# Forgetting attention: the value products of two heads in one group, alternating between the halves of the columns

## The chip, the cores and the metric

The kernel runs on one core of a Trainium2 chip. The metric is the time of one execution on the device in microseconds. The engines are TensorE (PE in the profile, its weight loads PEld), VectorE (DVE), ScalarE (ACT), GpSimd (POOL) and SyncE (SP), which issues most transfers.

## What is computed

The reference is one layer of a decoder trunk on 1024 tokens of width 1024: four token mixers side by side (RWKV-7, a convolution module, gated linear attention, forgetting attention), each projected up, gated and summed; then cross-attention and a SwiGLU feed-forward network. The change is in the forgetting attention (4 heads of width 64). Cut to what matters:

```python
qh = heads(f_q) * (FOX_HEAD_DIM ** -0.5)
kh, vh = heads(f_k), heads(f_v)
c = jnp.cumsum(log_f, axis=1).transpose(0, 2, 1)
for i in range(T // FOX_BLOCK):                 # 8 blocks of 128 queries
    q0, q1 = i * FOX_BLOCK, (i + 1) * FOX_BLOCK
    logits = jnp.einsum('bhtd,bhsd->bhts', qh[:, :, q0:q1], kh[:, :, :q1])
    logits = logits + c[:, :, q0:q1, None] - c[:, :, None, :q1]
    probs = softmax(where(mask, logits, -inf))  # causal
    outs.append(jnp.einsum('bhts,bhsd->bhtd', probs, vh[:, :, :q1]))
```

Query block i sees i + 1 key blocks of 128.

## The kernel before

Activations lie transposed, channels on partitions, in blocks of 128. Most matrix products are done in three products of high and low parts (`mm3`, L171, L174, L175), on 128 x 128 weights and 512 tokens. The products of the small mixers are plain float32.

**The heads.** `fox` (L862) works on two pairs of heads, p = 0 and 1. A pair's two heads, u = 0 and 1, have their values side by side in the columns of `vr` (fvr in the profile): columns 0 to 63 for u = 0, 64 to 127 for u = 1. `head` (L895) is a generator for 128 queries of one head in three steps:

- scores: three products (and a fourth, L907, for the causal mask) into `ps_fs`; then the softmax on VectorE and ScalarE: maximum (L911), its negation (L914), exponential with its sum (L917), reciprocal (L920), normalisation (L921) into `fp`;
- transposes: 128 x 128 blocks of `fp` on TensorE (L928, tile `ps_ft`), copied to `fpt` by ScalarE (L929);
- values: for each key block one product (L935) with a stationary operand of 128 rows and 64 columns, which lands in 64 partitions of `ps_fo`. Four query blocks of both heads share one bank, which ScalarE copies out (L939).

**What sets the order.** Sixteen such generators (8 query blocks, the two heads in turn) are run three deep: in step n the unit n - 2 does its values, n - 1 its transposes, n its scores, in this order on TensorE. `weave` (L204) puts FOX_PIECES = 4 pieces of fill ahead of each step. The fill is `gates` (L984): the gate and up projections of the branches that are finished, six matmuls a piece, with their weights' transfer (SP), cast (`whi`, ScalarE, L153) and low part (`wlo`, VectorE, L154). `queued` keeps a step's products behind the fill given out before. Inside these limits the framework's scheduler orders each engine's instructions.

**A place of the same shape.** In the gated linear attention, L784 forms the intra-chunk outputs: for each of four token blocks, one product for the head in columns 0 to 63 and one for the head in columns 64 to 127, in turn (tile `ps_oi`). Each of them is a sum by itself; nothing is added up over several.

`fp`, `fpt`, the queries, keys and values of a pair of heads share a pool of nine buffers (`pB`).

Of the kernel before, what the change touches and what calls it, by code (L numbers as in the profile page):

```python
# [22 lines left out]
P = 128  # L23
# [3 lines left out]
TH = 512  # L27
# [8 lines left out]
# blocks of w_in, in the order in which they are packed  # L36
# [5 lines left out]
# columns of the per-channel parameters  # L42
# [9 lines left out]
# columns of the constants  # L52
# [39 lines left out]
def hybrid_kernel(ctx, tc, io, out):  # L92
# [17 lines left out]
    def gps(name, shape=(P, TH), both=True):  # L110
        """one of four banks; the last two are left out unless both"""
        bank[0] = 1 - bank[0] if both else 0
        return psg.tile(list(shape), F32, tag=("g", "g2")[bank[0]], name=name)

# [49 lines left out]
    def mm3(ps, pairs, start=True, stop=True, lag=99):  # L164
        """ps (+)= sum of the products of (lhs hi, lhs lo, rhs hi, rhs lo), each exact to f32.

        The products of hi parts run lag pairs ahead of the others."""
        n = len(pairs)
        for i in range(n + min(lag, n)):
            if i < n:  # L170
                mm(ps, lhsT=pairs[i][0], rhs=pairs[i][2], start=start and i == 0, stop=False)  # L171
            if i >= min(lag, n):
                lh, ll, rh, rl = pairs[i - min(lag, n)]
                mm(ps, lhsT=ll, rhs=rh, start=False, stop=False)  # L174
                latest[0] = mm(ps, lhsT=lh, rhs=rl, start=False, stop=stop and i == n + min(lag, n) - 1)  # L175
        return latest[0]
# [3 lines left out]
    def queued():  # L180
        """what the tensor engine is given here comes after the products that were last given to it"""
        return tc.issue_after(latest[0].ins)

    def drain(gen, n=None):
        """n more steps of gen (all that are left when n is None)"""
        while n is None or n > 0:
            if next(gen, gen) is gen:
                return
            n = n if n is None else n - 1
# [4 lines left out]
    def both(gens):  # L194
        """two generators of two steps, side by side"""
# [8 lines left out]
    def weave(fill, streams, n=1, idle=0, gate=None):  # L204
        """the streams' steps in turn, behind n pieces of fill each; then idle more of these.

        A step that gives out a number waits until gate() has reached it."""
# [21 lines left out]
    def rstd(srcs, col, alloc, op, const, minus=(), order=ExitStack):  # L229
        """1/sqrt of op(sum over channels of srcs, const), in PSUM, on all channels; the square of the  # L230
        sum over channels of minus is taken off first.

        srcs [P, w] add up, col [P, heads] holds the channels' weights per head (a head is P // heads
        partitions). The root is taken with the tokens on partitions, and refined by a Newton step.
        In two steps.
        """
# [35 lines left out]
    # the tensor engine's clock rises while the first loads are under way  # L272
# [18 lines left out]
    def project(src, evac, w=None, pieces=1, both=True):  # L291
        """a block of x's projections, in pieces of each half's product"""
# [12 lines left out]
    # shifted r, k, v: per half [P, pair, TH]; the others over all tokens  # L305
# [29 lines left out]
    def rwkv(t1, ps1, fill):  # L335
# [9 lines left out]
        # lower-triangular score matrices, transposed; what lies outside the mask stays zero  # L345
# [4 lines left out]
        # DRAM images of [P, 4, P] matrices in which the 16 x 16 diagonal blocks have one stride  # L350
# [19 lines left out]
        def score(alloc, dst, m, ks, qs, cs, name):  # L370
            """masked scores of the four heads, keys on partitions"""
# [10 lines left out]
        def prepare(hf):  # L382
            """what a half needs before its state: a generator of steps; a step's number is given out
            first where it is about to write the chunk's scores"""
# [27 lines left out]
            # kmod takes the place of k, rk that of the squares, nb that of a  # L412
# [9 lines left out]
            # decays; kk, nb, kmod and r are scaled in place  # L422
# [4 lines left out]
            def scale(c):  # L427
                cs = slice(c * P, (c + 1) * P)
                q = pp([P, 2, 256], "ps_ce")
                # exact: the constants are 0 and +-1  # L430
# [25 lines left out]
            # inverses of I minus the diagonal blocks (both orientations)  # L456
# [15 lines left out]
        # heads are kept in the order h = 2 * (half of the partitions) + pair  # L472
        def chunk(hf, c, r, kk, nb, kmod, v, y, ecl, bm):
            """a chunk of 128 tokens in CHUNK steps"""
# [8 lines left out]
            # (I - A)^-1 and its transpose: blocks of 16 to 32, to 64, to 128  # L483
# [27 lines left out]
            # rows  # L511
# [35 lines left out]
            # U0 | W  # L547
# [29 lines left out]
            # next state  # L577
# [11 lines left out]
            # outputs, transposed  # L589
# [13 lines left out]
        def chunks(hf, args):  # L603
            """the chunks of a half; a chunk's first steps go with the last two of the one before"""
# [13 lines left out]
        def finish(hf, rk, v, xg, misc, y):  # L618
            # normalisation over a head's channels
# [12 lines left out]
            for p in range(2):  # L632
                # bonus, then the output gate
# [54 lines left out]
    def log_sigmoid(dst, x, tmp):  # L688
        """dst = min(x, 0) - log(1 + exp(-|x|))"""
# [172 lines left out]
    def fox(t2, ps2, c_d):  # L862
        for p in range(2):
# [21 lines left out]
            # three heads under way: scores, their transposes, the values  # L885
            zo = [None, None]
            units = [head(p, u, i, qa[u], ka[u], vr, zo, t2, ps2) for i in range(8) for u in range(2)]
# [7 lines left out]
    def head(p, u, i, qa, ka, vr, zo, t2, ps2):  # L895
        """128 queries of a head, in three steps"""
        n = (i + 1) * P
        qs = slice(i * P, n)
        us = slice(64 * u, 64 * u + 64)
# [24 lines left out]
        for j0 in range(0, i + 1, 4):  # L924
# [4 lines left out]
            nc.scalar.copy(pt[:, j0:j0 + m], z[:, 0:m])  # L929
        yield  # L930
        if u == 0 and i % 4 == 0:
            zo[i // 4] = ps2.tile([P, 4, P], F32, tag="gi", name="ps_fo", bufs=2)
        z = zo[i // 4]
        for j in range(i + 1):
            mm(z[us, i % 4], lhsT=vr[:, j, us], rhs=pt[:, j], start=j == 0, stop=j == i)  # L935
        if u == 1 and i % 4 == 3:
# [44 lines left out]
    merged = []  # L981

    def gates(br, t2):
        """a branch's part of the merge, in pieces"""  # L984
# [71 lines left out]
    class HL:  # L1056
        """hi and lo parts of a transposed activation, 8 blocks of [P, TH], of one half of the tokens."""
# [14 lines left out]
    class Norm:  # L1072
        """LayerNorm over the 1024 channels (8 blocks x partitions) of some of the tokens, in place.

        add(j) is called when block j is there; steps(sink) then goes on in small steps and calls
        sink(j, ap) after each block. eng adds up over the blocks.
        """
# [12 lines left out]
        def square(self, j, c, first):  # L1090
            """centre block j, square it; all but the first square are added to the first"""
# [18 lines left out]
        def steps(self, sink):  # L1110
            """a step for the mean, 8 for squares, one for the root, 8 for what is left"""
# [13 lines left out]
    class LastNorm(Norm):  # L1125
        """The same where nothing follows that could hide it: blocks are centred by the mean c of the
        first two as soon as that is known, and the variance is mean((x - c)^2) - mean(x - c)^2; its two
        terms are at most 4 and 3 times the variance, since c is the mean of a quarter of the channels."""
# [18 lines left out]
        def finish(self, dst):  # L1147
            last, acc = KD - 1, self.acc
            # the table of the root is loaded ahead of the need
# [21 lines left out]
    # w_out and the first norm; the norm of one half goes with the products of the next  # L1171
# [14 lines left out]
    # keys and values of mem, in units of one or two blocks of weights  # L1186
# [3 lines left out]
    def memory():  # L1190
# [9 lines left out]
        def load(n):  # L1200
            h, g = units[n]
            # more blocks are under way where w_out has made room
# [7 lines left out]
        for n, (h, g) in enumerate(units):  # L1210
# [11 lines left out]
            else:  # L1222
# [5 lines left out]
                # one bank, two sums: only its first product clears what is written  # L1228
# [37 lines left out]
    # cross-attention; a head's output takes the place of its queries  # L1266
    qh = [HL(pA, "A", "qA"), HL(pM, "M", "qB")]

    def attend(hf, h):
        """in steps; each step is sent the matrix product behind which its own are to queue"""  # L1270
# [34 lines left out]
    def gemms(items):  # L1305
        """output blocks of half the tokens, two pieces each: first pieces, then second pieces"""
# [47 lines left out]
    def run_head(unit, gen, n):  # L1354
        """the steps of a head, with n pieces of gen before each"""
# [37 lines left out]
    # SwiGLU; x2 accumulates alpha * x2 + its output  # L1393
# [5 lines left out]
    def ffn_up(f, sls, ws, steps=(0, 0)):  # L1399
        """the numbers of steps of side to go on after each of the two products"""  # L1400
# [16 lines left out]
    def ffn_down(fs, ws, sls, ln=None):  # L1417
        """adds the products of some blocks; those with the last block wait for a second output block"""
# [45 lines left out]
    # the last blocks by slices of the tokens, so that the norm of one goes with the products of the next  # L1464
# [22 lines left out]
def _pack(inp):  # L1487
# [30 lines left out]
    def tiles(m):  # L1518
        """[K, F] -> [F/128, 128, K/128 * 128]: the stationary blocks, contiguous."""
# [8 lines left out]
    # [4 heads * 2, 128, (4 k, 256)]  # L1528
# [3 lines left out]
    # [branch, 8 j, 128, (2 k, 128)]  # L1532
# [46 lines left out]
```

## Time and profile before

| | |
|---|---|
| timed runs, median of 3 | 2235.68 us (2231.76 to 2238.44) |
| span of the profiled execution, first to last instruction | 2235.5 us |
| TensorE busy | 2195.0 us, 98% |
| VectorE, ScalarE, GpSimd busy | 51%, 33%, 9% |
| value products of the forgetting attention (L935) | 144 products, which are 288 matmuls |
| from their first to their last start | 651.3 to 929.1 us |

The profiled execution has no time of its own beside its span; the runs were timed apart from it. Matmuls are pipelined, so the duration of one (start to end) is longer than the distance to the next start, and the sum of durations of a line is not its cost. What a group of matmuls costs is read from the starts: of the instruction before it, of its first, and of the instruction behind it.

### The profile page before, as it was taken

What the parts mean: (1) busy time and instruction counts of PE and PEld (TensorE: products, weight loads), DVE (VectorE), ACT (ScalarE), POOL (GpSimd) and SP (SyncE); (2) the same over time, 40 slices, a digit from 0 to 9 for tenths busy, and PEclk for the clock granted to TensorE, in tenths of its full rate; (3) what the DMA queues carried; (4) which work ended last, traced back from release to release, by engine and by line L of the source; (5) the groups of instructions that cost most, each with busy time, mean ns of one, the idle gap of its engine ahead of it and who ended that gap; (6) DMA issues with size and microseconds to landing.
All of it is one profiled execution on the core that took longest, in us unless ns stands there. A gap on an engine that the chain in (4) does not pass through costs nothing.

```text
span 2235.5 us, 28264 instructions
## 1 busy us (share of the span) xinstructions
PE 2195.0 (98%) x11468; PEld 1794.7 (80%) x11468; DVE 1149.8 (51%) x2004; ACT 727.2 (33%) x1165; POOL 209.6 (9%) x173
## 2 busy tenths in 40 slices
PE   9999999999999999999999999989999999999997
PEld 7878777777787878888888888877888888888787
DVE  4365287524444433333466346775455455445577
ACT  3343111126646555422234333342111111111223
POOL 0000000000001111121024000150000000000122
PEclk9999999999999999999999999999999999999999
DMA  6122121122211211111444102331111111111421
GB/s 205 48 74 82 51 85 49 62 100 89 62 56 60 68 56 41 37 55 48 132 130 149 43 29 95 99 99 57 48 57 47 48 47 53 51 38 58 148 78 48
DMA packets 87682, 161.08 MB, mean 72 GB/s; under 512 B 19606, under 2 KB 43848, under 8 KB 87552
## 3 DMA queue, kind: packets, MB, share of 16 engines
q1 hardware_dynamic: 87552, 159.28, 22.3%
q8 instruction: 90, 1.47, 0.3%
q14 instruction: 40, 0.33, 0.0%
HBM read 134.50 MB, written 24.76 MB: 71 GB/s over the span
## 4 chain that ended last, share of the span: by engine, by line
PE 91%; issue 3%; DVE 2%; POOL 2%; ACT 1%; DMA 1%; SPq 0%; DVEq 0%; POOLq 0%; ACTq 0%
PE ps_w L174 10%; PE ps_w L175 10%; PE ps_w L171 9%; PE ps_gate L171 5%; PE ps_gate L175 5%; PE ps_gate L174 5%; PE ps_g L171 4%; PE ps_g L175 4%; PE ps_g L174 4%; PE ps_q L174 2%; PE ps_q L175 2%; PE ps_q L171 2%; PE ps_fo L935 2%; PE ps_up L171 1%; PE ps_up L175 1%
## 5 line engine op out<-in xcount | busy, mean ns | idle before, releaser
L153 ACT CAST whi<-wraw 128x1024 fp32r<-128x1024 f32 x189 | 197.9, 1048 | 338.4 <-issue 212.5
L154 DVE TENSOR_TENSOR wlo<-wraw,whi 128x1024 fp32r<-128x1024 f32 x164 | 212.8, 1298 | 158.5 <-ACT whi L153 157.2
L175 PE MATMUL ps_gate<-xl,whi 128*128 128x512 f32 x512 | 200.8, 392 | 0.0
L174 PE MATMUL ps_gate<-xh,wlo 128*128 128x512 f32 x512 | 200.6, 392 | 0.0
L1431 DVE TENSOR_TENSOR x<-x,ps_w 128x512 f32<-128x512 f32 (+1 forms) x306 | 189.1, 673 | 11.0 <-PE ps_w L175 10.6
L171 PE MATMUL ps_gate<-xh,whi 128*128 128x512 f32 x512 | 165.4, 403 | 0.0
L174 PE MATMUL ps_g<-xh,wlo 128*128 128x512 f32 x400 | 158.3, 396 | 0.0
L175 PE MATMUL ps_g<-xl,whi 128*128 128x512 f32 x400 | 158.2, 396 | 0.0
L174 PE MATMUL ps_w<-x2B,wlo 128*128 128x512 f32 (+1 forms) x416 | 147.4, 365 | 3.6 <-POOL wlo L154 3.5
L175 PE MATMUL ps_w<-x2B,whi 128*128 128x512 f32 (+1 forms) x416 | 147.1, 364 | 0.0
L171 PE MATMUL ps_g<-xh,whi 128*128 128x512 f32 x400 | 140.4, 416 | 2.9 <-ACT xh L153 2.8
L175 PE MATMUL ps_w<-hl,whi 128*128 128x512 f32 (+1 forms) x384 | 140.9, 372 | 1.9 <-DVE hl L154 1.7
L174 PE MATMUL ps_w<-hh,wlo 128*128 128x512 f32 (+1 forms) x384 | 141.0, 372 | 0.0
L174 PE MATMUL ps_w<-x2A,wlo 128*128 128x512 f32 x352 | 137.5, 391 | 0.0
L175 PE MATMUL ps_w<-x2A,whi 128*128 128x512 f32 x352 | 137.4, 390 | 0.0
L154 POOL TENSOR_TENSOR wlo<-wraw,whi 128x1024 fp32r<-128x1024 f32 x25 | 63.2, 2528 | 776.4 <-ACT whi L153 770.4
L171 PE MATMUL ps_w<-hh,whi 128*128 128x512 f32 (+1 forms) x384 | 133.1, 372 | 1.0 <-ACT hh L153 1.0
L1414 DVE TENSOR_TENSOR hs<-hs,ps_w 128x512 f32<-128x512 f32 (+1 forms) x48 | 30.8, 642 | 177.2 <-PE ps_w L175 177.0
L174 PEld LDWEIGHTS ps_gate<-xh,wlo 128*128 128x128 f32 x512 | 96.6, 189 | 21.0 <-issue 0.6
L175 PEld LDWEIGHTS ps_gate<-xl,whi 128*128 128x128 f32 x512 | 96.6, 189 | 20.5
L171 PEld LDWEIGHTS ps_gate<-xh,whi 128*128 128x128 f32 x512 | 93.5, 190 | 20.5 <-issue 3.5
L1022 POOL TENSOR_TENSOR merged<-merged,gsig 128x512 f32<-128x512 f32 x48 | 66.1, 1376 | 406.2 <-DVE gsig L1021 301.0
(457 smaller groups left out, 4402.9 us busy)
## 6 DMA issues: line engine op xcount, KB each, us to landing
wraw<-ffn_w SPq DMA_DIRECT2D x84, 512.0 KB, 3.5
wraw<-wblk SPq DMA_DIRECT2D x57, 512.0 KB, 3.6
wraw<-xa_wo SPq DMA_DIRECT2D x16, 512.0 KB, 3.5
xraw<-xT SPq DMA_DIRECT2D x16, 256.0 KB, 6.1
yld<-y_d SPq DMA_DIRECT2D x16, 256.0 KB, 2.5
uraw<-ups SPq DMA_DIRECT2D x32, 128.0 KB, 2.9
wraw<-w_out SPq DMA_DIRECT2D x8, 512.0 KB, 3.5
xr<-xT SPq DMA_DIRECT2D x16, 256.0 KB, 4.4
```

Of the source, the lines that this page charges most:

```text
L153: nc.scalar.copy(hi, src)
L154: eng.tensor_tensor(out=lo, in0=src, in1=hi.bitcast(F32), op=ALU.subtract)
L171: mm(ps, lhsT=pairs[i][0], rhs=pairs[i][2], start=start and i == 0, stop=False)
L174: mm(ps, lhsT=ll, rhs=rh, start=False, stop=False)
L175: latest[0] = mm(ps, lhsT=lh, rhs=rl, start=False, stop=stop and i == n + min(lag, n) - 1)
L935: mm(z[us, i % 4], lhsT=vr[:, j, us], rhs=pt[:, j], start=j == 0, stop=j == i)
L1022: nc.gpsimd.tensor_tensor(out=mj, in0=mj, in1=sg, op=ALU.add)
L1414: tt(out=s, in0=s, in1=p[1], op=ALU.mult)
L1431: tt(out=x2[j][:, sl], in0=x2[j][:, sl], in1=ps, op=ALU.add)
```

## The change

`head` for u = 0 no longer does its values: it leaves its transposed probabilities in a list `pts`, and its third step is empty. The third step of u = 1 does the values of both heads: key block by key block, first the product of u = 0 into partitions 0 to 63, then that of u = 1 into partitions 64 to 127. The products, their operands, their sums and the bank are the same; comments and empty lines aside, nothing else is edited.

```diff
-            zo = [None, None]
-            units = [head(p, u, i, qa[u], ka[u], vr, zo, t2, ps2) for i in range(8) for u in range(2)]
+            zo, pts = [None, None], [None, None]
+            units = [head(p, u, i, qa[u], ka[u], vr, zo, pts, t2, ps2) for i in range(8) for u in range(2)]
...
-    def head(p, u, i, qa, ka, vr, zo, t2, ps2):
+    def head(p, u, i, qa, ka, vr, zo, pts, t2, ps2):
...
-        us = slice(64 * u, 64 * u + 64)
...
+        pts[u] = pt
         yield
-        if u == 0 and i % 4 == 0:
+        if u == 0:
+            yield
+            return
+        if i % 4 == 0:
             zo[i // 4] = ps2.tile([P, 4, P], F32, tag="gi", name="ps_fo", bufs=2)
         z = zo[i // 4]
         for j in range(i + 1):
-            mm(z[us, i % 4], lhsT=vr[:, j, us], rhs=pt[:, j], start=j == 0, stop=j == i)
-        if u == 1 and i % 4 == 3:
+            for w in range(2):
+                us = slice(64 * w, 64 * w + 64)
+                mm(z[us, i % 4], lhsT=vr[:, j, us], rhs=pts[w][:, j], start=j == 0, stop=j == i)
+        if i % 4 == 3:
```

On TensorE, in the first pair of heads, the steps with the values of the seventh query block (7 key blocks; `ps_ft` are the transposes of the next unit, `ps_fs` the scores of the one after, `ps_gate` the fill; L941 is the product line of the changed kernel):

```order
@@ -2248,5 +2242,4 @@
 L174 MATMUL ps_gate<-xh,wlo 128x512
 L175 MATMUL ps_gate<-xl,whi 128x512
-L935 MATMUL ps_fo<-fpt,fvr 64x128 x7
 L928 MATMUL ps_ft<-cst,fp 128x128 x7
 L171 MATMUL ps_fs<-fkh,fqh 128x512
@@ -2278,5 +2271,5 @@
 L174 MATMUL ps_gate<-xh,wlo 128x512
 L175 MATMUL ps_gate<-xl,whi 128x512
-L935 MATMUL ps_fo<-fpt,fvr 64x128 x7
+L941 MATMUL ps_fo<-fpt,fvr 64x128 x14
 L928 MATMUL ps_ft<-cst,fp 128x128 x8
 L171 MATMUL ps_fs<-fkh,fqh 128x512
```

The group of the first head is gone and its transposes' neighbours stand directly behind the fill; the group of the second head has twice as many products. It is the same at all eight query blocks of both pairs.

The scheduler also moves some instructions of the other engines. On VectorE, in the second pair of heads, ahead of the softmax of the last unit (u = 1, 8 key blocks), before:

```order
L154 TENSOR_TENSOR ul<-uraw,uh 128x256
L911 TENSOR_REDUCE fst<-ps_fs 128x1 x2
L154 TENSOR_TENSOR wlo<-wraw,whi 128x1024
L913 TENSOR_TENSOR fst<-fst 128x1
L914 TENSOR_SCALAR fst<-fst 128x1
```

A weight's low part stands between the two maxima and their joining. In the changed kernel, at the same place:

```order
L154 TENSOR_TENSOR ul<-uraw,uh 128x256
L154 TENSOR_TENSOR wlo<-wraw,whi 128x1024
L911 TENSOR_REDUCE fst<-ps_fs 128x1 x2
L913 TENSOR_TENSOR fst<-fst 128x1
L914 TENSOR_SCALAR fst<-fst 128x1
```

The weight's low part has moved ahead of the maxima. In each pair of heads there are two more places at which a weight's low part now stands ahead of a part of the softmax, both at the fourth query block.

## Rows read from the trace of the kernel before

**Rows 1.** The page: busy time, share of the span, instructions.
```profile
PE 2195.0 (98%) x11468; PEld 1794.7 (80%) x11468; DVE 1149.8 (51%) x2004; ACT 727.2 (33%) x1165; POOL 209.6 (9%) x173
```

**Rows 2.** Stretches: length, busy time of each engine (instructions), granted clock, transfers.
```profile
core 0: us, PE busy (x) PEld busy (x) DVE busy (x) ACT busy (x) POOL busy (x), PEclk, DMA share, GB/s
636.00:930.00 294.00, 294.00 (x1527) 237.06 (x1526) 114.50 (x248) 170.75 (x278) 37.77 (x29) 1.00 0.16 50
1216.00:1226.40 10.40, 7.36 (x46) 5.89 (x45) 9.44 (x12) 6.07 (x10) 7.71 (x7) 1.00 0.70 232
1226.40:1233.20 6.80, 5.88 (x25) 5.69 (x26) 4.82 (x6) 0.99 (x2) 3.09 (x2) 0.50 0.34 114
```

**Rows 3.** The tile ps_fo: ns min/median/max, first and last start, forms.
```profile
L935 PEld LDWEIGHTS ps_fo<-fpt,fvr x288: 132/137/137, 651.3 to 929.0; 128*64 128x64 f32 x144
L935 PE MATMUL ps_fo<-fpt,fvr x288: 272/273/323, 651.3 to 929.1; 128*64 128x128 f32 x144
```

**Rows 4.** Order of time, TensorE, 918 to 923: start, us, instruction.
```profile
918.75 0.39 PE L175 MATMUL ps_up<-yl,uh 128*128 128x512 f32 x1
919.07 1.96 PE L935 MATMUL ps_fo<-fpt,fvr 128*64 128x128 f32 x16
920.96 1.09 PE L928 MATMUL ps_ft<-cst,fp 128*128 128x128 f32 x8
```

**Rows 5.** Order of time, TensorE, transposes without value products ahead.
```profile
644.97 0.39 PE L175 MATMUL ps_up<-yl,uh 128*128 128x512 f32 x1
645.21 0.27 PE L928 MATMUL ps_ft<-cst,fp 128*128 128x128 f32 x1
```

**Rows 6.** Chain of waits, 860 to 935: start, us, what.
```profile
864.27 1.24 PE ps_fo L935 x10
...
919.14 1.89 PE ps_fo L935 x16
```

**Rows 7.** Order of time, TensorE, the gated linear attention's alternating products.
```profile
578.70 0.39 PE L174 MATMUL ps_gate<-xh,wlo 128*128 128x512 f32 x1
578.93 0.39 PE L175 MATMUL ps_gate<-xl,whi 128*128 128x512 f32 x1
579.25 1.09 PE L784 MATMUL ps_oi<-scm,kv 128*64 128x128 f32 x16
580.27 0.73 PE L171 MATMUL ps_gate<-xh,whi 128*128 128x512 f32 x2
```

**Rows 8.** Order of time, VectorE, softmax at 4, 6 and 8 key blocks.
```profile
837.93 0.49 DVE L921 TENSOR_SCALAR fp<-fp,fst 128x512 f32<-128x512 f32 x1
...
845.59 0.58 DVE L921 TENSOR_SCALAR fp<-fp,fst 128x512 f32<-128x512 f32 x1
...
880.07 0.62 DVE L921 TENSOR_SCALAR fp<-fp,fst 128x768 f32<-128x768 f32 x1
...
914.26 1.22 DVE L154 TENSOR_TENSOR wlo<-wraw,whi 128x1024 fp32r<-128x1024 f32 x1
...
918.98 0.75 DVE L921 TENSOR_SCALAR fp<-fp,fst 128x1024 f32<-128x1024 f32 x1
```

**Rows 9.** Order of time, TensorE, the transposes of these units.
```profile
840.87 0.66 PE L928 MATMUL ps_ft<-cst,fp 128*128 128x128 f32 x4
...
848.75 0.66 PE L928 MATMUL ps_ft<-cst,fp 128*128 128x128 f32 x4
...
882.93 0.87 PE L928 MATMUL ps_ft<-cst,fp 128*128 128x128 f32 x6
```

**Rows 10.** The page: weights' cast and split (mean ns), transfer (KB, us to landing).
```profile
L153 ACT CAST whi<-wraw 128x1024 fp32r<-128x1024 f32 x189 | 197.9, 1048 | 338.4 <-issue 212.5
L154 DVE TENSOR_TENSOR wlo<-wraw,whi 128x1024 fp32r<-128x1024 f32 x164 | 212.8, 1298 | 158.5 <-ACT whi L153 157.2
...
wraw<-wblk SPq DMA_DIRECT2D x57, 512.0 KB, 3.6
```

**Rows 11.** Order of time, SyncE, 905 to 916: the transfer's issue.
```profile
915.50 0.33 SPq L158 DMA_DIRECT2D wraw<-wblk  x1
```

## The prediction

> **What bounds the kernel now.** I read the page's busy shares first. TensorE is busy for 98% of the span [rows 1]; the reader is to see that no other engine comes near. That share is an average, so I next took the busy times of the stretch in which the forgetting attention runs, 636 to 930 us: TensorE is busy for all 294.00 of its 294 us, at the full 2.4 GHz (granted clock 1.00), VectorE for 114.50, ScalarE for 170.75 [rows 2]. Whatever TensorE is spared there comes off the end, as long as nothing else becomes late.
>
> Then the products of probabilities and values themselves. A float32 product is two weight loads and two matmuls, so the 144 products of this line are 288 matmuls; each takes 272 to 273 ns from start to end [rows 3], but they are pipelined, and what counts is the distance between starts. In the order of time, the last group of the second pair of heads that has transposes behind it (8 key blocks, 16 matmuls) starts 0.32 us behind the start of the matmul before it, and the transposes behind it start 1.89 us later [rows 4]. Where no such group stands in between, the transposes start 0.24 us behind the same kind of matmul [rows 5]. So a group of 8 blocks costs 0.32 + 1.89 - 0.24 = 1.97 us. The chain of waits gives the slope: a group of 10 matmuls takes 1.24 us, one of 16 takes 1.89 [rows 6], hence 0.65 / 6 = 0.108 us a matmul, 0.217 a key block. A group of m blocks costs 0.234 + 0.217 m: the constant is the price of going over from full-width products to half-width ones and back, the rest is the streaming.
>
> **What two halves in alternation cost.** This kernel already has such a place: the intra-chunk products of the gated linear attention (L784), which alternate between columns 0 to 63 and 64 to 127 with the same operand shapes (128 x 64 stationary, 128 x 128 moving, float32). At full clock 16 of them start 0.32 us behind the matmul before, and the next matmul starts 1.02 us after their first [rows 7]. The 16 in one half took 1.89 [rows 4]. With 0.23 us, the usual distance of that stream (578.70 to 578.93 [rows 7]), taken off, the alternating 16 cost 0.32 + 1.02 - 0.23 = 1.11 us, and the formula with m = 4 gives 1.10: four blocks of two heads for the price of four blocks of one. The two halves run side by side.
>
> The Trainium skill, page "TensorE: Matmul & The Clock Gate", section "Part 3: Packing small matmuls — row/col tiling", says that a weight load overlaps matmuls in flight only where its row group differs; here all loads use all 128 rows. By that rule a pair of loads (137 ns [rows 3]) would stand ahead of its pair of matmuls. The trace disagrees: eight pairs of loads, each pair 137 ns, are 1.10 us by themselves, and the 16 alternating products with all their loads took 1.02 [rows 7]. What the rule would make of the time is the third rival.
>
> **The sum.** Against the profiled execution: its span is 2235.5 us, and the median of the timed runs is 2235.68, 0.2 more; I take 2235.7.
>
> - The groups of the first head of each couple go, and those of the second head now carry both heads at the price of one. Removed: 16 groups, m = 1 to 8 in each of two pairs of heads: 2 x (8 x 0.234 + 36 x 0.217) = 3.7 + 15.6 = 19.4 us (rounded last), of which 3.7 is the going over and back and 15.6 the streaming. All of it is on TensorE, which waits for nothing there.
> - A doubled group costs 0.01 us more by the alternating one (1.11 against 1.10): 16 x 0.01 = +0.2 us. Its bounds are the price above and no overlap at all, since no row shows halves in alternation that also add up over several products: 0.108 us for each of the 288 matmuls as now. I take the nearest row, L784, which has the same shapes and the same two halves of one bank.
> - Lost cover. The transposes of the second head of a couple used to start behind a group; now they follow the fill products directly, 0.234 + 0.217 m earlier, while the softmax that they wait for is no faster. What the softmax leaves today, from the end of VectorE's normalisation (L921, [rows 8]) to the first transpose [rows 4, 9], is 2.58 us at m = 4 (846.17 to 848.75), 2.24 at m = 6 (880.69 to 882.93) and 1.23 at m = 8 (919.73 to 920.96). The cover that goes is 1.10, 1.54 and 1.97 us. So 1.48 and 0.70 stay, and at m = 8 a wait of 0.74 us opens, once for each pair of heads: +1.5 us. Behind the waiting transposes stand on TensorE the fill products, so all of it would be on the path. At the same place the change also moves the weight split (1.22 us at 914.26) from between the maximum of the scores and its negation to ahead of the maximum [rows 8]; if the split is done by then, the softmax is earlier by that and the wait is gone. Bounds 0 and 1.5; I take the middle, 0.7.
> - The scores follow the transposes closely and come earlier by the same amount in these steps; the scores' banks are freed by exponentials that lie ahead of L921, so they add no wait of their own. The held transposed probabilities take a buffer for one step more; at the doubled group all are read and free, and TensorE passes that group ahead of the scores whose exponentials need the buffer, so I cost this at nothing. If a buffer ran short, the exponential would wait for a group that is at most one step off, and it would show as a longer softmax, which is the last point again.
> - DVE, ACT and the transfers do the same work in 19 us less: ScalarE goes from 170.75 / 294 = 58% to 62%, VectorE from 39% to 42% [rows 2]. Nothing there becomes the bound.
>
> Sum: 2235.7 - 19.4 + 0.2 + 0.7 = 2217.2; predicted **2217 us**.
>
> What this sum can't fix: everything behind 930 us moves forward by some 19 us against the clock gate. At 1226.4 the granted clock falls to 1.2 GHz (0.50) for 6.80 us, behind a stretch in which TensorE was busy for 7.36 of 10.40 us [rows 2]; 5.88 us of work at half clock cost about 2.9. One such stretch more or less, or a longer one, is ±3 us; two of them ±6.
>
> **The rivals.**
> 1. *Halves that accumulate do not overlap.* Speaks for it: no row has alternation and accumulation together. Against: the one-half groups accumulate block by block at 0.108 us a matmul, no slower than streaming allows in L784. Then only the going over and back of 16 groups is saved: 2235.7 - 3.7 = 2232.
> 2. *The lost cover eats half.* If TensorE waits at all 16 places for as long as half the cover that it lost (19.4 in all), 9.7 us come back: 2227. For it: at m = 8 the reserve is below the loss. Against: at m = 4 and 6 it is above, and the smaller groups lose less than 1.1 us.
> 3. *The loads stand in line.* 144 pairs, each a load of 137 ns and then a matmul's 109: 0.246 x 144 = 35.4 against 288 x 0.108 = 31.1 now; +4.3, less 3.7 for the groups: 2236. It is the rule named above; [rows 7] speak against it.
> 4. *Slower: the weight splits that now stand ahead of softmax steps on VectorE hold them up.* This is so at three places in each pair of heads (both heads at m = 4, the second at m = 8). Were a weight's transfer issued only as the step begins, 3.6 us of landing, 1.05 of cast and 1.30 of split [rows 10] would be 5.95 us ahead of the softmax. The reserves are 2.45 (838.42 to 840.87, [rows 8, 9]; this place keeps its cover), 1.48 and -0.74, so TensorE would wait 3.50 + 4.47 + 6.69 = 14.7 us a pair, 29.3 in all: 2235.7 - 19.2 + 29.3 = 2246. It decides from an average wait of 3.2 us at a place on. Against it: the transfer of the next weight is issued at 915.50 [rows 11], as soon as the split begun at 914.26 has freed its buffer, so the data lie ready long before their cast.
>
> **How the numbers follow.** Forecast 0.86, first rival 0.05, second 0.04, third 0.02, fourth 0.03. The forecast's own range is 2212 to 2222: the waits 0 to 1.5 and the clock's ±3, a little widened. I give 2211 to 2226, which takes in two stretches of clock on the fast side and most of the way to the second rival. About 0.3% (6.7 us) is what a measurement of this kernel can tell from no change, so faster means below 2229 and slower above 2242.4. Faster: the forecast and half of the second rival, 0.88. Within: the first, the third and the other half of the second, 0.09. Slower: the fourth, 0.03.
>
> **What would show it.** In the changed profile, groups of 32 matmuls on the product line take the 1.89 us that 16 take now; starts come in close pairs 0.11 us apart; the line's busy time falls from 38 us to some 20; TensorE's idle time ahead of the transposes stays under 1.5 us in total; and the time from the first scores to the last group is shorter by 18 to 19.5 us, with nothing moved behind it but the clock's dips. I would be wrong by the first or third rival if a group of 32 takes over 3 us, by the second if the transposes show idle time released by L921 at many places, by the fourth if that idle time is released by a split or a transfer.

## The result, and the profile after

| | before | changed |
|---|---|---|
| median of the timed runs | 2237.06 us (2231.76 to 2244.91, 4 runs) | 2214.89 us (2212.85 to 2222.68, 4 runs) |
| span of the profiled execution | 2235.5 us | 2211.4 us |
| from the first scores' mask product to the last transposes' first start | 281.34 us | 261.61 us |

The ratio is 0.990, with an interval of 0.987 to 0.993: the change is faster, by about 1%. The prediction was 2217 us.

The page of the changed kernel, busy times as in [rows 1]:

```profile
PE 2173.6 (98%) x11468; PEld 1778.3 (80%) x11468; DVE 1149.4 (52%) x2004; ACT 727.0 (33%) x1165; POOL 212.6 (10%) x173
```

The counts of instructions are the same to the last one, and TensorE's share is still 98%: it has lost 21.4 us of busy time without having lost an instruction. The view of stretches shows where, first the whole forgetting attention (it ends some 18 us earlier than the stretch of [rows 2]), then the stretch of the table above; columns as in [rows 2]:

```profile
636.00:912.00 276.00, 275.66 (x1532) 224.40 (x1531) 116.91 (x249) 169.08 (x276) 41.82 (x30) 1.00 0.18 56
...
636.53:898.14 261.61, 261.27 (x1440) 212.34 (x1437) 113.45 (x245) 164.41 (x269) 39.13 (x28) 1.00 0.18 56
```

The same stretch of the kernel before, between the same two instructions (the mask product L907 and the first transposes L928 of the last unit):

```profile
639.62:920.96 281.34, 281.34 (x1455) 226.34 (x1452) 112.22 (x246) 166.23 (x270) 36.48 (x28) 1.00 0.16 52
```

Both are at the full clock (1.00), so 281.34 - 261.61 = 19.73 us is the change itself. TensorE is idle for 0.34 us of it where it was idle for nothing.

The other 24.1 - 19.7 = 4.4 us of the two spans lie outside: 3.1 ahead of the stretch, where the program is the same, and 1.3 behind it. Most of them go with the clock. TensorE stands at half clock in eleven short stretches before and in ten after. One of the kernel before (another is in [rows 2]):

```profile
7.83:14.65 6.82, 6.06 (x13) 4.24 (x14) 5.98 (x9) 5.53 (x10) 0.00 (x0) 0.50 1.03 377
```

and two of the changed kernel:

```profile
492.15:495.56 3.41, 3.41 (x10) 2.38 (x10) 1.45 (x7) 3.12 (x6) 0.00 (x0) 0.50 0.23 82
...
1205.53:1208.95 3.42, 3.42 (x18) 3.42 (x17) 2.25 (x4) 0.62 (x1) 1.40 (x1) 0.50 0.23 83
```

Added up, half clock takes 20.5 us ahead of the stretch before and 17.1 after; behind it, without the last 9 us of the span, 23.9 and 20.5. That is 3.4 us less on each side, worth about half of it, 1.7 us, each time; the other 1.0 of the 4.4 is not placed. What lies ahead of the stretch comes before any changed instruction, so these 3.1 us are what the two profiled executions happened to be granted and to wait, not what the change gave; of the 1.3 behind it that is likely, but not shown. The medians, which are 22.2 us apart, may hold some of it too.

The product line in the view of the tile, as in [rows 3]:

```profile
L941 PE MATMUL ps_fo<-fpt,fvr x288: 272/273/324, 654.3 to 906.3; 128*64 128x128 f32 x144
```

288 matmuls of the same 273 ns as before. A reader who multiplies count by duration finds no difference at all; the change is in the distances between starts. The line's busy time, in which matmuls that overlap count once, shows it as well, and falls as the prediction had said, from 38 us to some 20 (before, then after; busy us, mean ns):

```profile
L935 PE MATMUL ps_fo<-fpt,fvr 128*64 128x128 f32 x288 | 38.3, 278 | 0.0
```

```profile
L941 PE MATMUL ps_fo<-fpt,fvr 128*64 128x128 f32 x288 | 19.3, 278 | 0.0
```

The chain of waits shows the distances (start, length, what), answering to [rows 6]:

```profile
871.65 1.46 PE ps_fo L941 x24
...
888.60 1.68 PE ps_fo L941 x28
...
904.63 1.90 PE ps_fo L941 x32
```

32 matmuls now take the 1.90 us that 16 took (1.89), and the slope is 0.22 us for 4 matmuls, which was the price of 2. TensorE's order of time, answering to [rows 4]:

```profile
888.21 0.39 PE L175 MATMUL ps_gate<-xl,whi 128*128 128x512 f32 x1
888.53 1.75 PE L941 MATMUL ps_fo<-fpt,fvr 128*64 128x128 f32 x28
890.21 0.98 PE L928 MATMUL ps_ft<-cst,fp 128*128 128x128 f32 x7
```

The entry costs 0.32 us as before, and seven key blocks of two heads take 1.68 us to the transposes behind them.

### The profile page after: what moved, and what is told of

Same layout as the page of the kernel before. It is cut to its first block, busy times and chain, and to the rows that moved or that the text cites. A ratio compares the mean times of both kernels' runs of the same rounds, so it can differ in the third digit from the quotient of the medians.

```text
span 2211.4 us, 28249 instructions
## 1 busy us (share of the span) xinstructions
PE 2173.6 (98%) x11468; PEld 1778.3 (80%) x11468; DVE 1149.4 (52%) x2004; ACT 727.0 (33%) x1165; POOL 212.6 (10%) x173
## 4 chain that ended last, share of the span: by engine, by line
PE 90%; issue 3%; DVE 2%; POOL 2%; ACT 1%; DMA 1%; SPq 0%; DVEq 0%; ACTq 0%; POOLq 0%
PE ps_w L174 10%; PE ps_w L175 10%; PE ps_w L171 9%; PE ps_gate L171 5%; PE ps_gate L175 5%; PE ps_gate L174 5%; PE ps_g L171 4%; PE ps_g L175 4%; PE ps_g L174 4%; PE ps_q L174 2%; PE ps_q L175 2%; PE ps_q L171 2%; PE ps_up L171 1%; PE ps_up L175 1%; PE ps_up L174 1%
```

## The experiments

The measure in them is the stretch of the table above (281.34 before, 261.61 after), and in it the sum of the distances from the start of one value product's matmul to the next one's, which is free of the clock's dips elsewhere: 241 distances, 27.89 us before and 13.20 after. "Extra" below is against the changed kernel.

**Both heads in one group, but one after the other.** It keeps everything of the change except the alternation.

```diff
-        for j in range(i + 1):
+        for j0 in range(0, i + 1, 8):
             for w in range(2):
                 us = slice(64 * w, 64 * w + 64)
-                mm(z[us, i % 4], lhsT=vr[:, j, us], rhs=pts[w][:, j], start=j == 0, stop=j == i)
+                for j in range(j0, min(j0 + 8, i + 1)):
+                    mm(z[us, i % 4], lhsT=vr[:, j, us], rhs=pts[w][:, j], start=j == 0, stop=j == i)
```

> Both heads' value products in one group as in the changed kernel, but all key blocks of the first head, then all of the second. Measure: the stretch from the first mask product of the scores to the first of the last transposes, 281.34 us before and 261.61 after. Theory A (the two column halves work side by side, products start in the order of issue): only the last block of one head meets the first of the other, 16 x 0.217 = 3.5 of the 15.6 us of streaming stay saved, so the stretch is 261.6 + 12.1 = 273.7 and the time about 2227 us. Rival B (each change of half spares a fixed 0.109 us, as if only the weight load were hidden): 16 changes, 1.7 us saved, 275.5. Rival C (each half has a queue of its own that is filled far ahead): no loss, 261.6. Rival D (the gain is the halved number of groups and the scheduler's new order on the other engines, not overlap): no loss either, 261.6.

Measured: median 2227.97 us, ratio 0.996 (0.994 to 0.997); stretch 270.00, distances 21.63 us. None of the four forecasts is met: theory A had said 273.7, rival B 275.5, C and D 261.6. So fewer groups and the new order alone (D) are not the whole gain, and alternation is worth 8.4 us of the 19.7. But the kernel is also faster than two heads strictly one after the other would be: its distances are 6.3 us below those of the kernel before. The last group in the chain of waits:

```profile
916.68 3.26 PE ps_fo L942 x32
```

3.26 against 1.90 us is 1.36 more, or 1.36 / 0.217 = 6.3 key blocks out of 8 that no longer lie beside another: nearly two of the first head's blocks still overlap the second head. TensorE starts the second half while the first still has two blocks to go.

**Runs of two and of four.** The same edit, with 2 and with 4 in the place of 8.

> As the changed kernel, but the halves alternate every two key blocks. Theory A, worked out product by product with starts in order of issue and one product at a time in a half: the groups stream 19.0 us instead of 15.7, one key block more a group, stretch 261.6 + 3.3 = 264.9. Rival B (0.109 us per change of half): half the changes, 261.6 + about 7.8 = 269.4. Rival C: 261.6.

> As the changed kernel, but the halves alternate every four key blocks. Theory A: the groups stream 24.9 us instead of 15.7, stretch 261.6 + 9.2 = 270.8. Rival B: a quarter of the changes, 261.6 + 11.7 = 273.3. Rival C: 261.6.

Measured: runs of two 2219.96 us, ratio 0.992 (0.989 to 0.995), stretch 262.02, distances 13.68; runs of four 2224.26 us, 0.994 (0.993 to 0.996), stretch 266.65, distances 18.25. The last groups, of two in the order of time (1.95 us to the next start), of four in the chain:

```profile
909.23 2.02 PE L942 MATMUL ps_fo<-fpt,fvr 128*64 128x128 f32 x32
911.18 0.73 PE L171 MATMUL ps_up<-yh,uh 128*128 128x512 f32 x2
```

```profile
914.50 2.50 PE ps_fo L942 x32
```

Runs of two are all but free, which theory A did not allow: it let products start strictly in order, each as soon as its own half is free (runs of two: stretch 264.9). Theory A fell in this form. In its place: products are still passed on in order, but a half takes in the next product while one streams. Counted in key blocks, for a group of 8 blocks and two heads, the extra over strict alternation is then:

| run | no look-ahead | one product ahead | two ahead | measured in the last group |
|---|---|---|---|---|
| 2 | 1 | 0 | 0 | 0.2 (1.95 us) |
| 3 | 3 | 1 | 0 | 1.2 (2.17 us, next run) |
| 4 | 5 | 2 | 1 | 2.8 (2.50 us) |
| 8 | 7 | 6 | 5 | 6.3 (3.26 us) |

**Runs of three**, with which the new theory was tested, since it had been made from the other runs.

> As the changed kernel, but the halves alternate every three key blocks. The runs of 2, 4 and 8 cost less than the theory of products starting in the order of issue, one at a time in a half, had said. New theory A2: products are issued in order, but a half takes in the next product while one still streams in it, so two in a row in one half do not keep the other half waiting, and a third does. Worked out product by product, the starts within the groups ahead of the last transposes (13.2 us in the changed kernel, 18.25 with runs of 4) add up to 16.3 us. One at a time in a half: 20.1. Two ahead instead of one: 13.7.

A single run: 2216.8 us, where the kernel before took 2234.52 on the same chip; distances 16.17 us. The last group:

```profile
911.61 2.17 PE ps_fo L942 x32
```

16.17 is where one product ahead puts it (16.3), far from no look-ahead (20.1) and from two ahead (13.7). In the single groups the measured extra lies 0.2 to 0.8 block above the table, runs of four the most. So "one product" is the nearest whole number, not an exact law: a float32 product is two matmuls, and counted in matmuls the measured values lie between a half that holds three and one that holds four. The 16.3, too, can be argued with: worked out again at 0.109 us a matmul from the 13.20 of strict alternation, one product ahead gives 15.6, none 19.5 and two 13.2; one ahead stays the nearest by far. The starts in the trace show where the halves first meet in the last group: the second half's first matmul starts 0.006 us behind the 13th of the first half's 16 matmuls with runs of eight, behind the 5th of 8 with runs of four, behind the 3rd of 6 with runs of three, and 0.014 us behind the 1st of 4 with runs of two. Each time three matmuls of the first run were still to start. (The records don't name the half; it is told by the two rows of starts, each 0.109 us apart.)

**The alternating products twice.** If the products stand on the path with the price read, doubling them must lengthen the kernel by that price.

```diff
-        for j in range(i + 1):
+        for j in [*range(i + 1)] * 2:
```

> As the changed kernel, but each group's alternating products are issued twice, the second pass starting the sums anew, so the output is the same. Theory A: 144 products more in pairs, 72 x 0.217 = 15.6 us more, all of it on the path since TensorE is the bound: stretch 277.2, less up to 0.5 us of wait that the longer groups cover; time about 2230 us. If another engine bounded this stretch after the change, the added products would partly vanish in TensorE's idle time and the stretch would grow by clearly less than 15 us.

Measured: 2231.11 us, ratio 0.997 (0.996 to 0.999); distances 27.17 us, that is 13.97 more, and 1.74 more in the last group, which lies behind the stretch: together the 15.7 expected. The stretch itself, 275.18, came out 2 us below the expected 277.2: 1.7 since the expectation counted the last group into it, 0.3 since the one wait ahead of the transposes shrank from 0.50 to 0.19 us. 144 more products added 15.7 us: 0.109 a product, 0.217 a key block of both heads.

**The control: the kernel before with each group twice in one half.**

> The kernel before, with each head's group of value products issued twice, the second pass starting the sums anew, so the output is the same. 288 matmuls more at 0.109 us, one after the other: the stretch from the first scores to the last transposes grows by 31.4 less the last group's 1.7, from 281.3 to 311.0 us, twice what the doubled alternating groups cost. If the halves overlapped across groups anyway, it would grow by less.

A single run: 2264.79 us; stretch 310.94 (expected 311.0), that is 29.6 more (31.3 with the last group), twice what the same 144 products cost in alternation. The largest groups of the two experiments, in the order of time, first the alternating one with two heads twice, then the one-half one with one head twice:

```profile
919.87 3.71 PE L941 MATMUL ps_fo<-fpt,fvr 128*64 128x128 f32 x64
```

```profile
956.34 3.71 PE L935 MATMUL ps_fo<-fpt,fvr 128*64 128x128 f32 x32
```

64 matmuls in alternation and 32 in one half take the same 3.71 us.

**Three pieces of fill in the place of four**, in the changed kernel and in the kernel before (`FOX_PIECES = 3`), to see how near the lost cover has brought the softmax.

> The changed kernel with three pieces of fill ahead of each step of the forgetting attention instead of four; the pieces left over come later. A piece is six matmuls, 1.36 us, and covers the softmax. In the changed profile the transposes have 0.15 to 3.46 us of reserve; where it is under 1.36 they would wait. Theory: the change has spent the reserve, and TensorE waits about 7.8 us in all ahead of the transposes (sum of 1.36 less the reserve over the eleven places below 1.36), most of it at the second head of a couple. Rival: the cover that the change took away was not needed, the softmax simply moves along, and the waits stay below 2 us.

> The kernel before with three pieces of fill ahead of each step. Its reserves ahead of the transposes are 1.23 us and more, so with 1.36 less cover it waits 0.1 us at two places, below 1 us in all, if the reserve is what the change has spent; several us, like the changed kernel, if both kernels have the same reserve.

Single runs: 2220.95 and 2239.79 us. The view of waits over 630 to 930 us (us in total, times, longest), changed kernel, then the kernel before:

```profile
PE ps_ft L928 <- DVE fp L921: 1.8, 7, 0.4
```

```profile
PE ps_ft L928 <- DVE fp L921: 0.4, 1, 0.4
```

With a piece less, the changed kernel waits for the softmax at 7 places and the kernel before at one: the reserve has indeed been spent. But by starts these waits come to about 2.8 us, between the 7.8 expected and the rival's 2. The likely reason is that the scheduler rearranged the other engines' work again; that is not shown. Both kernels are 5 to 6 us slower than with four pieces (2220.95 against 2214.89, 2239.79 against 2234.52 on the same chip), so that loss isn't the change's. With four pieces, the reserve from the end of L921 to the transposes is 1.23 us or more at all 32 places in the kernel before; in the changed kernel it is under that at ten, and between 0.15 and 0.19 us at three of them.

**The same in RWKV-7.** Its state and output products (L582 to L597) have 64-column halves too, `us`, but go head by head, and heads 0 and 1 lie in one half, 2 and 3 in the other, so that two heads' products stand in one half before the other's turn. Regrouped by kind, with the halves in turn; each half is now started (`start`) by its first product alone, where each head's sum was:

```diff
-            for h in range(4):
-                us = slice(64 * (h // 2), 64 * (h // 2) + 64)
-                p = h % 2
-                mm(q[us, p], lhsT=bk[:, p, us], rhs=UW[:, h, 0:64], start=True, stop=False)
-                mm(q[us, p], lhsT=bk[:, 2 + p, us], rhs=vh(h), start=False, stop=first)
...
+            hp = [(h, h % 2, slice(64 * (h // 2), 64 * (h // 2) + 64)) for h in (0, 2, 1, 3)]
+            for h, p, us in hp:
+                mm(q[us, p], lhsT=bk[:, p, us], rhs=UW[:, h, 0:64], start=p == 0, stop=False)
+            for h, p, us in hp:
+                mm(q[us, p], lhsT=bk[:, 2 + p, us], rhs=vh(h), start=False, stop=first and p == 1)
...
```

> The changed kernel, and in each of the eight chunks of the RWKV mixer the products of the next state (ps_s) and of the outputs (ps_y) regrouped: all four heads' first products with the column halves in turn, then their second ones, then the third ones with 64 rows, instead of head by head. In the changed kernel the starts of these lines add up to 46 us, with one half at a time and a going over between 128-row and 64-row products in every head. Theory (halves side by side, and each going over costs): about 2.75 us a chunk, 22 us, so 24 us less, time about 2191 us. Rival: the RWKV chunks wait on their own chain of small steps rather than on TensorE, and half of it or more turns into TensorE waiting: 2203 or above.

Measured: 2192.88 us (5 runs), ratio to the kernel before 0.980 (0.979 to 0.982), 22 us less than the changed kernel. The starts of these two groups of products go from 46.0 to 19.7 us in all (expected: to 22, 24 less; it was 26.3 less), and the profiled span is 25.1 us shorter. In the order of time, kernel before, the third of a chunk's four heads and the first product of the fourth, state:

```profile
226.26 0.33 PE L582 MATMUL ps_s<-UW,bk 128*64 128x64 f32 x2
226.43 0.28 PE L583 MATMUL ps_s<-vr,bk 128*64 128x64 f32 x2
226.64 0.33 PE L585 MATMUL ps_s<-S,GT 64*64 64x64 f32 x2
226.89 0.33 PE L582 MATMUL ps_s<-UW,bk 128*64 128x64 f32 x2
```

0.63 us a head, 2.5 for four. In the regrouped kernel, all four heads:

```profile
220.97 0.40 PE L175 MATMUL ps_g<-xl,whi 128*128 128x512 f32 x1
221.30 0.45 PE L581 MATMUL ps_s<-UW,bk 128*64 128x64 f32 x8
221.58 0.40 PE L583 MATMUL ps_s<-vr,bk 128*64 128x64 f32 x8
221.91 0.45 PE L585 MATMUL ps_s<-S,GT 64*64 64x64 f32 x8
222.29 0.66 PE L592 MATMUL ps_y<-ArbT,UW 128*64 128x128 f32 x8
```

0.99 us for the four heads' state (221.30 to 222.29). More than half goes. The change of form between 128-row and 64-row products is now also paid once for four heads and not once for each, which would account for that; no run separates the two.

**That, and a third buffer for the branches' outputs.** In the changed kernel TensorE still has one wait in the fill behind the attention (order of time):

```profile
957.41 0.50 PE L171 MATMUL ps_up<-yh,uh 128*128 128x512 f32 x1 [1.70 <-ACT yh L153]
```

The cast there waits for a transfer that has only two buffers (`yld`).

```diff
-                t = t2.tile([P, TH], F32, tag="yld", name="yld")
+                t = t2.tile([P, TH], F32, tag="yld", name="yld", bufs=3)
```

> The kernel with the regrouped RWKV products, and three buffers instead of two for the branch outputs that the gates load again (yld). In the changed profile TensorE stands for 1.7 us at 956 us, since the third of four such loads starts only when the first is split. Theory: this wait shrinks or goes at the last branch, at most 2 us less than without it, about 2189; it can't be told by the time alone, only by the wait in the trace.

Measured: 2189.09 us (4 runs), ratio to the kernel before 0.978 (0.976 to 0.980); the wait is gone from the view of waits. That is some 4 us below the runs without it, but the two intervals overlap, and the profiled spans go the other way (2186.3 without it, 2188.7 with it), so only the wait is shown gone, not that it gave any of the 4 us. It has the lowest median here, 26 us below the changed kernel.

## Why the prediction was right

**TensorE sets the end: right.** 19.73 us fewer on TensorE in the stretch came off the span in full, 0.2 more than the 18 to 19.5 that the prediction named as its sign.

**A group of two heads costs what one head's did: right.** Predicted -19.4 + 0.2 for the 16 groups. By starts, the distances between products went from 27.89 to 13.20, which is 14.7. The other 5.0 lie around 16 groups: 16 x 0.203 = 3.2 from the last product to the transposes or scores behind it, 16 x (0.318 - 0.227) = 1.5 at the entries, 0.6 within the transposes and 0.3 around the scores' products, less a wait of 0.5. The group of 32 at 1.90 us is as L784 had promised [rows 7]. What no row had shown, that halves which add up over several products overlap all the same, is shown by the doubled products: 0.109 us each in alternation, 0.217 in one half. With it the first rival (2232) falls, and the third (2236): loads standing in line would have made a pair of matmuls 0.246 us, and the two pairs of a key block take 0.217 together.

**The going over and back, 0.234 a group: right, and it can now be placed.** Usual starts of full-width matmuls in the stream are 0.227 us apart, and a group's first matmul starts 0.318 behind such a one; in one half the second starts 0.160 behind the first where 0.109 is usual; the instruction behind the group starts 0.203 behind its last matmul, again against 0.109. In sum 0.09 + 0.05 + 0.09 = 0.23. One more piece was not in the working: the second of the transposes behind a group starts 0.166 us behind the first instead of 0.109, 0.06 a group, 0.6 us over the stretch (0.61 measured in the transposes).

**The waits at 8 key blocks, +0.7 (0 to 1.5): the size was in range, the place was wrong, so that the size came out is luck.** No transposes of 8 blocks wait. The term rests on a softmax as long as before, and that does not hold: at the second head of the second pair 0.56 and 1.99 us of reserve are left at 4 and 6 key blocks, where the prediction had 1.48 and 0.70, and at 8 there is 1.59 in place of a wait. VectorE in the second pair (order of time), answering to [rows 8], and TensorE:

```profile
890.28 2.00 DVE L154 TENSOR_TENSOR wlo<-wraw,whi 128x1024 fp32r<-128x1024 f32 x1 [0.21 <-ACT whi L153]
892.20 1.30 DVE L911 TENSOR_REDUCE fst<-ps_fs 128x1 f32<-128x512 f32 x2
...
895.79 0.76 DVE L921 TENSOR_SCALAR fp<-fp,fst 128x1024 f32<-128x1024 f32 x1
```

```profile
897.91 0.39 PE L175 MATMUL ps_up<-yl,uh 128*128 128x512 f32 x1
898.14 1.03 PE L928 MATMUL ps_ft<-cst,fp 128*128 128x128 f32 x8
```

The normalisation ends at 896.55, 1.59 us ahead of the transposes (1.33 in the first pair), where 1.23 were left before, although a cover of 1.97 has gone: from the mask product to the end of L921 the softmax takes 4.0 us and not 6.4. The prediction had named half of the reason as one of its bounds: the weight's split is done before the maxima start (1.22 us at 914.26 in [rows 8] stood behind them). The other half is on ScalarE, in the order of time, kernel before:

```profile
915.81 1.28 ACT L917 ACT_TABLE_LOAD   x1 [1.99 <-DVE fst L914]
```

and changed kernel:

```profile
892.05 1.28 ACT L917 ACT_TABLE_LOAD   x1
893.91 0.69 ACT L917 ACTIVATE fp<-ps_fs,fst 128x512 f32<-128x512 f32 x1 [0.58 <-DVE fst L914]
```

The load of the exponential's table used to start behind the negated maximum; now it runs beside the maxima, and only the exponential waits. Of the 2.3 us by which this softmax is shorter (6.35 less 4.01), the split's move gave 1.0 and the table's load 1.3. What the prediction had not looked for is the mirror of the split's move elsewhere. TensorE at three key blocks, second head, second pair:

```profile
817.73 0.39 PE L175 MATMUL ps_up<-yl,uh 128*128 128x512 f32 x1
818.45 0.52 PE L928 MATMUL ps_ft<-cst,fp 128*128 128x128 f32 x3 [0.34 <-DVE fp L921]
```

and what VectorE did ahead of that:

```profile
813.85 0.54 DVE L911 TENSOR_REDUCE fst<-ps_fs 128x1 f32<-128x384 f32 x1
814.32 1.21 DVE L154 TENSOR_TENSOR wlo<-wraw,whi 128x1024 fp32r<-128x1024 f32 x1
815.45 0.14 DVE L914 TENSOR_SCALAR fst<-fst 128x1 f32<-128x1 f32 x1
815.51 0.68 DVE L154 TENSOR_TENSOR yl<-yld,yh 128x512 fp32r<-128x512 f32 x1
...
817.89 0.42 DVE L921 TENSOR_SCALAR fp<-fp,fst 128x384 f32<-128x384 f32 x1
```

Here, in the new order, a split of 1.21 us stands between the maximum and its negation, and the transposes start 0.72 us behind the matmul before them, 0.5 more than usual. So the fourth rival's mechanism exists, at one place in 32 and for 0.5 us, not at six for 29: the data of the splits were there in time. It is not one of the places that the text ahead of the prediction had named: in the trace, of the two in each pair of heads, one is here, at three key blocks, and the other, where a split now stands ahead of the reciprocal, is at four; both are the second head's. In the first pair the same new order leaves 0.41 us at three key blocks, so a second wait was near. The second rival (half of the cover lost, 9.7 us) is out by the only wait of L928 in the stretch (us in total, times, longest):

```profile
PE ps_ft L928 <- DVE fp L921: 0.3, 1, 0.3
```

**The sum.** 19.73 measured against 19.4 - 0.2 - 0.7 = 18.5, 1.2 more: the wait was 0.2 us smaller than its term, the doubled groups did not cost the 0.2 that they were given, the transposes gave 0.6 and the scores' products 0.3 that no term had. What is left between 2217 and 2214.89 is within what the clock's dips were given (±3).

## What to carry to other kernels

Where two streams of TensorE products use 64 columns each, give them out alternately, in runs of at most two: the second stream was then all but free here, also where each half accumulates, and the change of form is paid once for both. That is shown for float32 products with 128 moving columns, and in RWKV-7 with 64. Look for it in starts or in the line's busy time, not in count times duration, which is the same in the two kernels; a place in the same kernel that already alternates gives the price beforehand. After such a change the cover of everything behind the moved products shrinks, so read the reserve at each place, and look in the new order for long instructions that have come to stand inside short dependent chains.

## What the runs showed that was not expected

- A half needs no strict alternation: over the stretch, runs of two cost 0.5 us more (13.68 against 13.20), runs of three 3.0, of four 5.1, of eight 8.4. It fits a half that takes in about one product ahead while one streams.
- The change between full-width and half-width products is paid at four places: 0.09 us at the entry, 0.05 behind the first matmul, 0.09 at the exit and 0.06 within the transposes that follow.
- Weight loads of 137 ns take no time of their own in alternation, though all use the same 128 rows: 32 loads and their 32 matmuls in 1.90 us.
- ScalarE's table load, 1.28 us, stood behind a wait for VectorE or beside it, as the order of the other engines fell out; at the last softmax it was worth 1.3 us, the split that the change had moved 1.0.
